# A two-layer attention and state-space decoder: state parameters in ten hooked parts, state data in longer runs, memory values token-major, first channels by contraction tile, norm rows in f32r

## The chip, the cores and the metric

One core of one Trainium2 chip runs the whole program. The metric is the device time of one execution in microseconds (us), as the median of several runs. The engines are TensorE (PE, with its weight loads PEld), VectorE (DVE), ScalarE (ACT), GpSimd (POOL) and SyncE (SP). SP computes nothing here: it issues every transfer of the kernel, in one order fixed at build time.

## The reference

512 tokens of width 1024 pass two layers, and each layer has three residual blocks. Cut to what matters:

```python
for l in range(DEPTH):                                   # 2
    xn = rmsnorm(h, norm_mix_g[l])
    c_q, c_kv, k_r, u = jnp.split(xn @ w_in[l], split_at, axis=-1)
    a_out = mla_group(c_q, c_kv, k_r, ...)               # 8 heads, causal, low-rank q and kv, rotary
    s_out = s5_group(u, lam, log_dt, b, c, d, w_glu, b_glu)
    h = h + concat(rmsnorm(a_out), rmsnorm(s_out)) @ w_out[l]
    h = h + memory_cross_attention(rmsnorm(h), rmsnorm(mem), w_xq, w_xkv, w_xo)   # 256 memory tokens, 4 heads
    h = h + swiglu(rmsnorm(h), w_gate, w_up, w_down)     # inner width 2816
return rmsnorm(h, final_norm_g)

def s5_group(...):                                       # 32 groups of 16 channels, 64 complex states each
    a_bar = jnp.exp(lam * dt); b_bar = ((a_bar - 1) / lam) * b
    states = associative_scan(x[t] = a_bar * x[t-1] + b_bar @ u[t])
    y = Re(c @ states) + d * u; g = gelu(y)
    return y * sigmoid(g @ w_glu + b_glu)
```

## The kernel before

**Layout.** Activations lie channel-major: 128 channels on the partitions, 512 tokens along the free axis, eight such tiles for the width. Every float32 product is three f32r products: each operand is split into a rounded part (`hi`, by ScalarE) and a rest (`lo`, by VectorE, a few by GpSimd), and TensorE adds hi*hi, hi*lo and lo*hi (`mm3`, lines 213 to 218). A weight block is a 128x1024 tile, 512 KB: one transfer into `wraw`, one ScalarE pass (`whi`, L208), one VectorE pass (`wlo`, L209), 24 matmuls, each of them with two buffers.

**Norms.** A norm's row statistics are a column of sums (L289), a scale (L292), a power on GpSimd (L294), and a row that is copied to all partitions (`row`, L276): float32 matmuls of the broadcast column with the identity, two records in the trace for each block of 128 tokens.

**The order of work.** The program is written in source order with priorities, and a planner fixes the order of each engine's queue at build time: an instruction's priority is its place in the source plus an offset (`later`, `OFFS`, `P_OFF`, `PR_UP`, `MS_UP`), and a tile gets a buffer of its tag when one comes free. The state-space work is cut into parts and hung between the 17 attention units `u` by `PLAN` (`x` memory keys and values, `v` state inputs, `m` direct terms, `c` scan, `y` outputs, `G` gelu, `g` gated unit, `s` norm). A part with a negative `u` comes ahead of the units.

**State parameters.** `s5_params` makes, from 1072 columns of parameters per partition, the powers of `a_bar`, the input matrices `BT` (four blocks q, L499, L510), the output matrices `dCA` (four blocks q, L499, L526, with the direct terms by L535), the direct table `dQ` (L541, L542) and the turning table `tab` (L555 to L559). Most of it is VectorE work: products of 128x512 (the helper `bmul`, L562, and the sum, L499). It is called once ahead of layer 0's attention, and once from layer 0's feed-forward block, after the first chunk, for layer 1. While it runs it holds the buffers of tag `s5b`, of which there are six, for parameters and three work tiles; in layer 0 also two for `BT`, which stays on the chip there (in layer 1 it goes through DRAM).

**State data.** The state channels `u` go to DRAM as `du` (L603) and come back as `U2` (L610, eight transfers of 128 KB) with a part of the time steps on the partitions; `U2` has tag `s5b`. The scan's result goes to `W` (L830), the outputs go through `dy` (L868) to `yS` (L872).

**Memory keys and values.** `xkv` makes 16 channel-major blocks of 128x256; VectorE scales them by the memory's norm row (L928). In the cross attention `v_tile` turns the values to token-major by four transposes for each of four tiles (L1036) and splits the result.

**The start.** `load_h` issues eight 256 KB tiles of x with the first weight block of `w_u` behind the first of them; `in_proj` then makes the four blocks of `u` one after the other, each over all eight contraction tiles.

## Time and profile before

| | us |
|---|---|
| median of 3 runs (1619.24 to 1625.9) | 1624.83 |
| the profiled execution | 1616.62 |
| its span, first to last instruction | 1614.8 |
| TensorE busy | 1516.8 (94%) |
| VectorE busy | 914.7 (57%) |
| ScalarE busy | 617.0 (38%) |
| GpSimd busy | 155.0 (10%) |

TensorE's busy time counts pipelined matmuls whose ends are modelled, so 94% doesn't mean that 94% of its best rate is reached: the granted clock of a stretch (1.00 is 2.4 GHz, 0.50 is 1.2 GHz) has to be read beside it. The span falls into these stretches: up to 66 us the first norm and the input projection; 66 to 275 us layer 0's attention with the state-space work; to 380 us its output projection, and the cross attention's start; to about 480 us the rest of the cross attention; to 840 us the feed-forward block; then the same for layer 1, whose attention runs from about 905 to 1070 us.

### The profile page before, as it was taken

To read this page: it belongs to the slowest core of one execution; us is meant where nothing else is said; L and a number is where in the kernel's file an instruction comes from. 1 tells how busy PE (TensorE), PEld (TensorE's weight loads), DVE (VectorE), ACT (ScalarE), POOL (GpSimd) and SP (SyncE) were. 2 spreads that over 40 slices of the span, in tenths; PEclk is the share of its full clock that TensorE was granted. 3 is DMA by queue.
4 is the path that set the end of the run, shared out by engine and by line. 5 is a ranking of instruction groups with operands and counts; after the bars stand their busy time and mean duration, and the time that the engine had idled before them with its cause. 6 is when DMAs were issued, how large, how long until landed. Compare 5 with 4: busy or idle time off the path is not lost.

```text
span 1614.8 us, 20187 instructions
## 1 busy us (share of the span) xinstructions
PE 1516.8 (94%) x8070; PEld 1259.5 (78%) x8070; DVE 914.7 (57%) x1278; ACT 617.0 (38%) x987; POOL 155.0 (10%) x110
## 2 busy tenths in 40 slices
PE   8868898998999999999998889989999999999997
PEld 6647777787878888888886778768888888888886
DVE  6996445757795534445454864555555553443554
ACT  5444365444333223223332455733444322222233
POOL 4310001101001100101100100110000110010111
PEclk9979999999999999999999799989999999999998
DMA  6266634221353222232349363322212223233222
GB/s 219 83 100 128 125 100 156 93 78 53 118 153 107 92 97 99 85 111 92 102 139 169 94 135 110 128 90 92 66 52 88 95 92 104 92 98 98 92 90 75
DMA packets 97630, 169.08 MB, mean 105 GB/s; under 512 B 32640, under 2 KB 55680, under 8 KB 97536
## 3 DMA queue, kind: packets, MB, share of 16 engines
q1 hardware_dynamic: 97536, 167.79, 35.6%
q8 instruction: 63, 1.03, 0.3%
q14 instruction: 31, 0.25, 0.1%
HBM read 150.00 MB, written 15.66 MB: 103 GB/s over the span
## 4 chain that ended last, share of the span: by engine, by line
PE 77%; DVE 7%; DMA 5%; ACT 2%; issue 2%; SPq 2%; POOL 1%; POOLq 0%; ACTq 0%; DVEq 0%
PE mm L215 13%; PE mm L217 13%; PE mm L216 13%; PE f L215 7%; PE f L217 7%; PE f L216 7%; PE mm L744 2%; ACT whi L208 1%; PE f L846 1%; DMA s5b<-dQ 1%; PE t L736 1%; DVE lo L238 1%; DVE wlo L209 1%; DMA wraw<-w_xkv 1%; POOL stat L294 1%
## 5 line engine op out<-in xcount | busy, mean ns | idle before, releaser
L208 ACT ACTIVATE whi<-wraw 128x1024 fp32r<-128x1024 f32 (+1 forms) x234 | 243.3, 1042 | 645.9 <-PE mm L216 299.3
L209 DVE TENSOR_TENSOR wlo<-wraw,whi 128x1024 fp32r<-128x1024 f32 (+2 forms) x228 | 316.5, 1388 | 96.2 <-ACT whi L208 93.9
L215 PE MATMUL mm<-hi,whi 128*128 128x512 f32 x589 | 230.6, 391 | 0.3 <-ACT whi L208 0.3
L217 PE MATMUL mm<-hi,wlo 128*128 128x512 f32 x589 | 229.4, 391 | 0.4 <-DVE wlo L209 0.4
L216 PE MATMUL mm<-lo,whi 128*128 128x512 f32 x589 | 229.3, 390 | 0.0
L215 PE MATMUL mm<-ghi,whi 128*128 128x512 f32 (+1 forms) x368 | 145.7, 396 | 9.2 <-ACT whi L208 7.8
L215 PE MATMUL f<-ghi,whi 128*128 128x256 f32 (+2 forms) x432 | 143.8, 333 | 6.3 <-DVE s5b L928 2.6
L217 PE MATMUL mm<-ghi,wlo 128*128 128x512 f32 (+1 forms) x368 | 145.6, 396 | 2.0 <-DVE wlo L209 1.9
L216 PE MATMUL mm<-glo,whi 128*128 128x512 f32 (+1 forms) x368 | 144.7, 394 | 0.2 <-DVE glo L238 0.2
L217 PE MATMUL f<-ghi,wlo 128*128 128x256 f32 (+2 forms) x432 | 142.5, 330 | 0.8 <-DVE wlo L209 0.8
L216 PE MATMUL f<-glo,whi 128*128 128x256 f32 (+2 forms) x432 | 142.4, 330 | 0.0
L215 PEld LDWEIGHTS mm<-hi,whi 128*128 128x128 f32 x589 | 110.5, 188 | 24.9 <-ACT whi L208 2.2
L217 PEld LDWEIGHTS mm<-hi,wlo 128*128 128x128 f32 x589 | 110.5, 188 | 24.0 <-DVE wlo L209 0.8
L216 PEld LDWEIGHTS mm<-lo,whi 128*128 128x128 f32 x589 | 110.5, 188 | 23.4 <-DVE lo L241 0.5
L1082 POOL TENSOR_TENSOR tmp<-tmp,tmp 128x512 f32<-128x512 f32 x44 | 60.4, 1373 | 573.7 <-DVE tmp L1081 517.4
L215 PE MATMUL f<-hi,whi 128*128 128x512 f32 (+1 forms) x293 | 114.9, 392 | 0.3 <-ACT whi L208 0.3
L217 PE MATMUL f<-hi,wlo 128*128 128x512 f32 (+1 forms) x293 | 114.5, 391 | 0.1
L216 PE MATMUL f<-lo,whi 128*128 128x512 f32 (+1 forms) x293 | 114.4, 390 | 0.0
L933 DVE TENSOR_TENSOR s5b<-mm,s5b 128x512 f32<-128x512 f32 x52 | 35.8, 690 | 114.7 <-PE mm L217 95.2
L237 ACT ACTIVATE hi<-tmp 128x512 fp32r<-128x512 f32 (+1 forms) x100 | 62.8, 630 | 96.4 <-POOL tmp L1082 59.7
L215 PEld LDWEIGHTS f<-ghi,whi 128*128 128x128 f32 (+1 forms) x432 | 82.0, 190 | 16.1 <-DVE tmp L1076 2.8
L215 PEld LDWEIGHTS mm<-ghi,whi 128*128 128x128 f32 (+1 forms) x368 | 69.9, 190 | 25.4 <-ACT whi L208 8.3
(278 smaller groups left out, 2623.6 us busy)
## 6 DMA issues: line engine op xcount, KB each, us to landing
wraw<-w_gate SPq DMA_DIRECT2D x44, 512.0 KB, 3.2
wraw<-w_up SPq DMA_DIRECT2D x44, 512.0 KB, 3.2
wraw<-w_xkv SPq DMA_DIRECT2D x32, 512.0 KB, 3.3
wraw<-w_down SPq DMA_DIRECT2D x30, 448.0 KB, 3.3
wraw<-w_out SPq DMA_DIRECT2D x16, 512.0 KB, 3.3
wraw<-w_xq SPq DMA_DIRECT2D x16, 512.0 KB, 3.2
wraw<-w_xo SPq DMA_DIRECT2D x16, 512.0 KB, 3.2
wraw<-w_down SPq DMA_DIRECT2D x16, 512.0 KB, 3.2
```

What stands on the lines that cost most here:

```text
L208: nc.scalar.activation(hi, raw, AF.Copy)
L209: (eng or nc.vector).tensor_tensor(lo, raw, hi.bitcast(F32), ALU.subtract)
L215: self.nc.tensor.matmul(ps, wh, xh, start=i == 0, stop=False)
L216: self.nc.tensor.matmul(ps, wh, xl, start=False, stop=False)
L217: last = self.nc.tensor.matmul(ps, wl, xh, start=False, stop=i == n - 1)
L237: a = nc.scalar.activation(hi, src, AF.Copy)
L238: b = eng.tensor_tensor(lo, src, hi.bitcast(F32), ALU.subtract)
L294: nc.gpsimd.tensor_tensor(col, ms, self.mhalf[:, :nb], ALU.pow)
L736: nc.tensor.transpose(pt[:, x * 128:(x + 1) * 128], p[ii][:, kb * 128:(kb + 1) * 128], self.ident)
L744: nc.tensor.matmul(po[64 * x:64 * x + 64, cs], vs[kb][:, (2 * pair + x) * 64:(2 * pair + x + 1) * 64], PT[x][:, kk * 256:min(n, kk * 256 + ...
L933: self.nc.vector.tensor_tensor(self.hs[m], ps, self.hs[m], ALU.add)
L1082: nc.gpsimd.tensor_tensor(uf, uf, gf, ALU.mult)
```

## The change

- `s5_params` becomes a generator of ten parts (`s5_gen`): part 0 the powers, parts 1 to 4 the blocks of `BT`, parts 5 to 8 those of `dCA` with their direct terms, part 9 `dQ` and `tab`. In layer 0 parts 0 to 4 stand where all stood, part 5 goes to `u` = -1 and parts 6 to 9 to `u` = 1. For layer 1 the parts hang behind the first gate and up blocks of the feed-forward (`FPLAN`), not behind the first chunk. `BT` goes through DRAM in both layers. Each block q of the direct terms has its own PSUM bank and copy. In layer 1 half of the second-half products of blocks 1 and 3 go to GpSimd (`POOLQ`). The rotary table's four work tiles move from `s5b` to tag `P`.
- `du`, `U2`, `W`, `dy` and `yS` get new layouts: the contiguous runs of `U2`'s load grow from 256 B to 1 KB, those of `W` from 256 B to 2 KB, those of `yS` from 256 B to 512 B; those written to `dy` shrink from 4 KB to 512 B. The number of transfers stays.
- The values of the memory are made token-major: the memory tile is the stationary operand, 256 value columns move. ScalarE scales the result by column, and `v_tile` splits it as it lies, without transposes.
- In layer 0, `w_u0` holds the `u` weights by contraction tile; `in_proj` runs over the contraction tiles with four PSUM banks open, and the four weight transfers stand between the x tiles.
- `row` splits the column into f32r parts (one ScalarE and one VectorE instruction of 128x4) and does two f32r matmuls for each block.
- `PLAN`, `OFFS`, `P_OFF`, `MS_UP` and `IN_POOL` get other values.

```diff
+    out["w_u0"] = wi[0][:, u0:].reshape(4, 2, 128, 512).transpose(0, 2, 1, 3).reshape(4, 128, 1024)
-    POOLQ = ((), ())
-    P_OFF = (150, 2900)
+    POOLQ = ((), (1, 3))
+    P_OFF = (500, 3000)
-    IN_POOL = ((0, 2, 6), ())
+    IN_POOL = ((2, 5), (3, 6))
     PLAN = ((
-        (-1, "x", 0), (-1, "x", 1), (1, "v", 0), (2, "m", 0), (2, "x", 2), (2, "m", 1), (2, "x", 3), (3, "m", 2),
+        (-4, "p", 0), (-4, "p", 1), (-4, "p", 2), (-4, "p", 3), (-4, "p", 4), (-1, "x", 0), (-1, "p", 5),
+        (-1, "x", 1), (-1, "x", 2), (1, "p", 6), (1, "p", 7), (1, "p", 8), (1, "p", 9), (1, "v", 0), (2, "m", 0),
 ...
-        (-2, "v", 0), (-2, "m", 0), (-1, "c", 0), (-1, "c", 1), (0, "m", 1), (0, "x", 0), (0, "x", 1), (0, "y", 0),
+        (-2, "v", 0), (-2, "m", 0), (-1, "m", 1), (-1, "x", 0), (-1, "x", 1), (0, "c", 0), (0, "c", 1), (0, "x", 2),
 ...
+    FPLAN = (0, 0, 1, 1, 1, 1, 1, 1, 2, 5)
-    PR_UP, MS_UP = 1500, 3000
+    PR_UP, MS_UP = 1500, 2300
     def row(self, col):
+        hi, lo = (self.t([128, 4], "cs", F32R)[:, :nb] for _ in range(2))
+        nc.scalar.activation(hi, col, AF.Copy)
+        nc.vector.tensor_tensor(lo, col, hi.bitcast(F32), ALU.subtract)
         for b in range(nb):
-            self.nc.tensor.matmul(ps[:, b * 128:(b + 1) * 128], col[:, b:b + 1].to_broadcast([128, 128]), self.ident,
-                                  start=True, stop=True)
+            for x in (hi, lo):
+                nc.tensor.matmul(ps[:, b * 128:(b + 1) * 128], x[:, b:b + 1].to_broadcast([128, 128]), self.identr,
+                                 start=x is hi, stop=x is lo)
     def rope_tables(self):
-        w = self.t([128, 4, 512], "s5b")
-        posf, ang, k, r = (w[:, i] for i in range(4))
+        posf, ang, k, r = (self.t([128, 512], "P") for _ in range(4))
     def s5_gen(self, l):
-        if l == 0:
-            BT = [x[:, q] for x in [self.t([128, 2, 2, 512], "s5b") for _ in range(2)] for q in range(2)]
-        else:
-            BT = self.dram([4, 128, 2, 512], f"dBT{l}")
+        BT = self.dram([4, 128, 2, 512], f"dBT{l}")
 ...
+            yield
     def in_proj(self, l):
+            for k in range(KT):
+                if k % 2 == 0:
+                    wh, wl = self.pre.pop(0)
+                for m in range(4):
+                    ms = slice((k % 2 * 4 + m) * 128, (k % 2 * 4 + m + 1) * 128)
+                    for w, x in ((wh, 0), (wh, 1), (wl, 0)):
+                        nc.tensor.matmul(pss[m], w[:, ms], X[k][x], start=k == x == 0 and w is wh,
+                                         stop=k == KT - 1 and w is wl)
     def load_u(self, du):
-            nc.sync.dma_start(U2[b * 16:(b + 1) * 16],
-                              du[:, :, 7 - b, :].rearrange("(g c) t j -> c t g j", c=16))
+            nc.sync.dma_start(U2[b * 16:(b + 1) * 16], du[:, 7 - b, :].rearrange("(g c) w -> c g w", c=16))
     def xkv(self, l, X, i):
+                    nc.tensor.matmul(o, xh[:, ts], wh[:, ks], start=hf == tb == k == 0, stop=False)
 ...
+            nc.scalar.activation(self.xv[:, tb, (i - 4) * 256:(i - 3) * 256], ps[:, tb * 256:(tb + 1) * 256], AF.Copy,
+                                 scale=self.mcol[:, tb:tb + 1])
         def v_tile(half, tb):
-            pt = self.p("t")
-            for i in range(4):
-                nc.tensor.transpose(pt[:, i * 128:(i + 1) * 128],
-                                    self.xv[:, half * 4 + i, tb * 128:(tb + 1) * 128], self.ident)
-            return self.split(pt)
+            return self.split(self.xv[:, tb, half * 512:(half + 1) * 512])
```

## Rows read from the trace of the kernel before

**Rows 1.** Windows: stretch and length; busy PE, PEld, DVE, ACT, POOL; clock; DMA share; GB/s.

```profile
0.00:66.00 66.00, 55.50 (x238) 43.32 (x239) 53.00 (x103) 28.93 (x46) 30.64 (x25) 0.95 0.49 168
66.00:132.00 66.00, 42.39 (x363) 32.41 (x362) 56.49 (x91) 29.71 (x57) 6.40 (x5) 0.77 0.59 108
132.00:275.00 143.00, 132.92 (x960) 113.88 (x959) 81.30 (x122) 73.04 (x141) 5.08 (x4) 0.98 0.49 121
380.00:500.00 120.00, 111.73 (x660) 92.34 (x659) 96.86 (x157) 46.66 (x78) 7.78 (x7) 0.97 0.37 114
500.00:850.00 350.00, 349.38 (x1545) 288.12 (x1544) 163.87 (x167) 100.65 (x122) 28.73 (x22) 1.00 0.31 102
850.00:905.00 55.00, 45.93 (x301) 36.96 (x300) 26.61 (x39) 17.28 (x30) 2.38 (x2) 0.84 0.81 157
905.00:1080.00 175.00, 157.81 (x1052) 134.66 (x1052) 103.44 (x156) 93.67 (x177) 16.45 (x6) 0.93 0.41 112
```

**Rows 2.** The chain that ended last, 104 to 132 us: start, length, what.

```profile
107.16 3.17 DMA dCA<-s5b
110.46 0.64 SPq L610
...
115.19 10.10 DMA s5b<-du
...
125.48 1.83 PE s L799 x29
```

**Rows 3.** VectorE's groups by form, 60 to 132 us: busy, mean ns, idle before.

```profile
L499 DVE TENSOR_TENSOR s5b<-s5b,tmps 128x512 f32<-128x512 f32 x16 | 10.7, 680 | 0.0
L562 DVE TENSOR_TENSOR s5b<-s5b,s5b 128x512 f32<-128x512 f32 x8 | 6.5, 816 | 0.0
L562 DVE TENSOR_TENSOR tmps<-s5b,s5b 128x512 f32<-128x512 f32 x8 | 5.9, 741 | 0.0
L558 DVE TENSOR_TENSOR tmps<-s5b 128x512 f32<-128x512 f32 x4 | 4.2, 1041 | 0.0
L555 DVE TENSOR_TENSOR s5b<-s5b 128x1024 f32<-128x1024 f32 x2 | 3.7, 1900 | 0.0
...
L292 DVE TENSOR_SCALAR stat<-t 128x4 f32<-128x4 f32 x2 | 0.3, 148 | 0.0
```

**Rows 4.** The chain that ended last, 856 to 908 us.

```profile
878.07 10.09 DMA tmps<-memT
...
889.59 0.69 DVE tmp L637
```

**Rows 5.** DMA issues of the whole span: count, KB each, median us to landing.

```profile
s5b<-xT SPq DMA_DIRECT2D x2, 1024.0 KB, 7.0
```

**Rows 6.** Windows of the start, columns as in the first group.

```profile
19.10:25.90 6.80, 6.80 (x19) 5.54 (x20) 4.27 (x9) 1.04 (x1) 6.12 (x4) 0.50 0.43 134
```

**Rows 7.** TensorE in order of time, 343 to 347 us: start, length, what.

```profile
343.00 1.05 PE L276 MATMUL t<-const,stat 128*128 128x128 f32 x8
343.88 0.60 PE L1036 MATMUL t<-const,s5b 128*128 128x128 f32 x4
344.24 0.47 PE L217 MATMUL mm<-hi,wlo 128*128 128x512 f32 x1
```

**Rows 8.** TensorE in order of time, 104 to 107.5 us.

```profile
105.09 0.22 PE L716 MATMUL s<-maskr,identr 128*128 128x128 f32 x1
105.15 0.44 PE L217 MATMUL mm<-hi,lo 128*128 128x512 f32 x1
```

**Rows 9.** ScalarE's groups by form, whole span: the smallest copy.

```profile
L325 ACT ACTIVATE identr<-const 128x128 fp32r<-128x128 f32 x1 | 0.3, 298 | 0.0
```

**Rows 10.** SP's waits, 380 to 480 us: total us, times, longest.

```profile
SPq L517 <- ACT tmps L516: 27.5, 7, 11.3
```

**Rows 11.** VectorE in order of time, 84 to 92 us.

```profile
88.53 1.77 DVE L562 TENSOR_TENSOR s5b<-s5b,s5b 128x512 f32<-128x512 f32 x1
```

**Rows 12.** Line 238 on GpSimd: duration ns min/median/max, first and last start us.

```profile
L238 POOL TENSOR_TENSOR lo<-tmp,hi x4: 1311/1576/4692, 85.5 to 916.9; 64x512 fp32r<-64x512 f32 x4
```

More of the change, by code (lines that the diff above doesn't have):

```diff
@@ L126, in lay_out @@
     out["w_xq"] = np.stack([blocks(v["w_xq"][l]) for l in range(L)])
-    out["w_xkv"] = np.stack([blocks(v["w_xkv"][l]) for l in range(L)])
+    out["w_xkv"] = np.stack([blocks(v["w_xkv"][l][:, :DM]) for l in range(L)])
+    xv = v["w_xkv"][:, :, DM:].reshape(L, 2, 4, 128, 4, 256)
+    out["w_xv"] = xv.transpose(0, 4, 1, 3, 2, 5).reshape(L, 8, 128, 1024)
     out["w_xo"] = np.stack([blocks(v["w_xo"][l]) for l in range(L)])
@@ L404, in s5_params, with s5_gen @@
     def s5_params(self, l):
+        gen = self.s5_gen(l)
+        return lambda i: next(gen)
+    def s5_gen(self, l):
         nc, V, P = self.nc, self.nc.vector, self.nc.gpsimd
@@ L607, in load_u @@
         nc = self.nc
-        U2 = self.t([128, 4, 8, 64], "s5b")
+        U2 = self.t([128, 8, 256], "s5b")
         for b in range(8):
-            nc.sync.dma_start(U2[b * 16:(b + 1) * 16],
-                              du[:, :, 7 - b, :].rearrange("(g c) t j -> c t g j", c=16))
-        self.U2 = U2.rearrange("p t g j -> p (t g) j")
+            nc.sync.dma_start(U2[b * 16:(b + 1) * 16], du[:, 7 - b, :].rearrange("(g c) w -> c g w", c=16))
+        self.U2 = [U2[:, q % 8, q // 8 * 64:q // 8 * 64 + 64] for q in range(G)]
     def in_proj2(self, l, X, R):
@@ L809, in s5_scan @@
         if hf == 0:
-            self.W = self.t([128, 32, 64], "s5b")
+            self.W = self.t([128, 2, 1024], "s5b")
         hs = slice(hf * 8, hf * 8 + 8)
@@ L836, in s5_y0 @@
         if q == 0:
-            self.y = self.t([128, 32, 64], "s5b")
+            self.y = self.t([128, 8, 4, 64], "s5b")
         if q % 2 == 0:
@@ L853, in s5_y @@
         if q == 0:
-            self.dy = [self.dram([128, 16, 64], f"dy{l}_{i}") for i in range(2)]
+            self.dy = [self.dram([128, 8, 128], f"dy{l}_{i}") for i in range(2)]
         y, half = self.y, q // 2
@@ L867, in s5_y @@
         dy = self.dy[half]
[L868 removed]
+        hs = slice(half * 128, half * 128 + 128)
+        nc.sync.dma_start(dy, y.rearrange("p g t j -> p g (t j)")[:, :, hs])
         if half == 0:
[L870 removed]
+            self.yS = self.t([128, 8, 256], "s5b")
         for g8 in range(8):
[L872 to L873 removed]
+            nc.sync.dma_start(self.yS[g8 * 16:(g8 + 1) * 16, :, hs],
+                              dy.rearrange("(s c) g w -> g c s w", c=16)[g8])
     def s5_gelu(self, l):
@@ L1136, in run @@
                 self.rope_tables()
-                self.s5_params(0)
+                params = self.s5_params(0)
+                for u, f, i in self.PLAN[0]:
+                    if u == -4:
+                        self.part(params, i, self.OFFS[0].get("p", 0))
             with (self.later(-self.PR_UP) if l == 0 else nullcontext()):
                 self.load_u(du)
+                if l == 0:
+                    for u, f, i in self.PLAN[0]:
+                        if u == -3:
+                            self.part(params, i, self.OFFS[0].get("p", 0))
                 self.in_proj2(l, X, R)
@@ L1154, in run, with hook @@
             self.cross(l)
-            self.ffn(l, lambda: self.s5_params(l + 1) if l + 1 < self.depth else None)
+            params = self.s5_params(l + 1) if l + 1 < self.depth else None
+            def hook(u):
+                for i, x in enumerate(self.FPLAN if params else ()):
+                    if x == u:
+                        self.part(params, i, 0)
+            self.ffn(l, hook)
         self.final()
```

126 lines of the change are left out of this document (69 added, 57 removed), and 10 rows, old and new, of the table PLAN.

## The prediction, made before the changed kernel ran

> **What bounds the kernel now.** I read the page's shares first: TensorE is busy for 94% of the span, so the end is set by its work and by what it loses. The windows [rows 1] say where it loses: busy time times granted clock is work at 2.4 GHz, and the rest of the stretch is lost. In the feed-forward, 500 to 850 us, 349.38 of 350 us at clock 1.00 are work; nothing is to be had there but by taking matmuls away. From 66 to 132 us it is 42.39 x 0.77 = 32.6 of 66 us, so 33 us are lost, the densest loss of the kernel; VectorE is busy for 56.49 of the same 66. From 132 to 275 us 132.92 x 0.98 = 130 of 143 are work, 13 lost. Layer 1's start loses 55 - 45.93 x 0.84 = 16 and its attention 175 - 157.81 x 0.93 = 28. The kernel's start, 0 to 66 us, loses 66 - 55.50 x 0.95 = 13. All other stretches together are small. The chain of waits, read next, names the causes. At layer 0 it runs over VectorE to the last `dCA` transfer (107.16 + 3.17 = 110.33), and only then over eight loads of `U2` (from 110.46 to 115.19 + 10.10 = 125.29) to the state matmuls at 125.48 [rows 2]. `U2` needs nothing of `dCA`; it needs a buffer of the six `s5b` ones, all of which the parameters hold, and SP stands with it. At layer 1 the chain goes over transfers that queue one behind another: a memory tile takes 10.09 us to land, and a VectorE evacuation at 889.59 stands behind its split [rows 4].
>
> **Layer 0's attention, 66 to 275 us.** Three edits meet here. `BT` and the rotary table leave `s5b`, so `U2` finds a buffer when `du` is there. The memory tiles and `x` parts come ahead of most of the parameters. And parts 5 to 9 move behind the first attention units. What moves on VectorE: half of the 16 sums (8 x 0.680 = 5.4 us), the second pass's 16 products (6.5 + 5.9), the table (4.2 + 3.7), together 25.7 us [rows 3], plus small ones. It is not removed: in the new place 25.7 us are added to a stretch where VectorE is busy for 81.30 of 143. So I don't add up stalls, I ask how well the joined stretch can be filled. TensorE's work in it is 32.6 + 130 = 163 us, in 209 us: 78%. VectorE's is 56.49 + 81.30 = 138 us. Two rows show what TensorE reaches beside a busy VectorE: 91% from 132 to 275 us, with VectorE at 57%, and 90% from 380 to 500 us (111.73 x 0.97 of 120) with VectorE at 96.86 of 120, or 81%, under the same parameter work [rows 1]. At 87% the stretch takes 163/0.87 = 187 us and VectorE stands at 74%. That is 22 us less. I take a little under the two rows because the state chain (`v`, `m`, `c`, `y`) now starts behind later parameters. Bounds: 163/0.91 = 179 us, 30 less, and nothing; a loss is the slower rival's, below. What hides the moved work is the 17 us or so of `x` products, three parts of 48 matmuls, and the attention units; if that cover isn't ready, the stall comes back at `u` = 1. The new transfers of `BT`, eight out and eight in, queue on SP ahead of weight loads; I cost them at nothing while two weight tiles lie ready, and price the rest as a rival.
>
> **Longer runs, layer 1's start.** `U2` takes 125.29 - 110.46 = 14.8 us for 1 MB in 256 B runs [rows 2]; 1 MB of x in 2 KB runs lands 7.0 us after its issue [rows 5]. With 1 KB runs I take 6 us less, between 0 and 7.8. In layer 0 that is inside the sum above. In layer 1, 850 to 905 us, the DMA engines are busy for 0.81 of the time [rows 1] and the memory tile waits behind `U2` [rows 4], so I carry 5 us to the end. The loads of `W` and `yS` gain too, the write to `dy` loses its 4 KB runs; SP's issues stay in number. From 905 to 1080 us I take 3 us for these and for `x` parts at -1. Together -8, bounds -17 (both stretches filled to 87%: 185/0.87 = 213 of 230 us) and +4 (the shorter runs of `dy`, and `c` behind -1, delaying `y`).
>
> The Trainium skill, page "DMA: Bandwidth & Descriptors", Specifications, says that transfers under 512 B fall short of line rate and gives some 358 GB/s for a core's HBM side. By that, as an estimate, 1 MB in 1 KB runs would take 3 us instead of 14.8 and layer 1 would gain some 6 us more than I take: 1582 instead of 1588. The trace doesn't agree with that rate here: 1 MB took 7.0 us even in 2 KB runs [rows 5].
>
> **The start.** `u` by contraction tile lets TensorE take 12 matmuls per x tile instead of 3. But it already starts on the first tile, so only the stretch at 1.2 GHz from 19.1 to 25.9 us [rows 6] can go: 6.8 x 0.5 = 3.4 us, and some waits. Against it stand 512 KB weights between the x tiles and one `lo` pass more on VectorE. I take -3, bounds -6 and +2.
>
> **Values token-major.** The products stay the same in number and width. 32 transposes go: eight groups of four, each from 343.88 to 344.24, 0.36 us of TensorE's stream [rows 7]: 8 x 0.36 = -2.8 us, at full clock and in the path. The scale moves from VectorE to two ScalarE copies, hidden while ScalarE is busy for under half. Bounds -2.8 and -1.
>
> **Norm rows.** Now eight records take 343.88 - 343.00 = 0.88 us [rows 7]. An f32r product of 128 columns takes 105.15 - 105.09 = 0.06 us at best [rows 8], so eight take 0.48, at worst the same 0.88. For 14 rows that is 0 to -5.6; I take -3. The two new instructions (at most 0.298 and about 0.148 us [rows 3, 9]) with two hand-overs add some 0.5 us to the norm's chain, and ScalarE's queue may stand before them. This shows only where TensorE waits for the row, at four places: the attention norm of both layers and the two last norms: 4 x 0.5 = +2. Net -1, bounds -4 and +6.
>
> **Layer 1's parameters.** Their `BT` writes already stand between 380 and 480 us [rows 10], ahead of the feed-forward in whose source they are called: the planner runs them when an engine is free, and an earlier place changes little. GpSimd takes 12 products from VectorE: 12 x 0.68 = 8 us less in a stretch at 81%, beside slower POOL work. I take 0, bounds -6 and +9.
>
> **Sum.** -22 - 8 - 3 - 2.8 - 1 + 0 = -36.8 us. The profiled execution took 1616.62 us (its span 1614.8), so it would take 1579.8. The median of the runs is 8.2 us above it; with the same distance the changed kernel's median is 1588. The terms' bounds, not all at once, make 1568 to 1602.
>
> **Rivals.**
>
> *The stall only moves.* Parts 6 to 9 stand together at `u` = 1, and TensorE's queue holds their matmuls in order, as it did before; if the joined stretch reaches 82% instead of 87%, it takes 199 us and gains 10: 1600. For it: 25.7 us of VectorE work in a row. Against: the row of 90% beside the same work.
>
> *The buffers don't come free.* Parameters with three work tiles, `U2` and the attention's output make six; the first key tile then finds no `s5b` buffer until part 8 is through, and the `x` cover is missing. Then only the wait for `U2` goes, some 12 us: 22 - 12 = 10 us worse, 1598. For it: that is just how `U2` waits now. Against: the attention's output is first written late.
>
> *GpSimd slows VectorE.* Beside GpSimd's work a product took 1.77 us instead of 0.68 [rows 11], and a GpSimd pass took 4.692 us at worst instead of 1.311 [rows 12]. If all 12 products went like that, 12 x 4.692 = 56 us, in which VectorE does 0.68/1.77 of its work, it would lose 35 us, less the 8 that it is spared: +27 if none of its slack in that stretch takes it up, so 1615. The Trainium skill, page "GPSIMD Engine Reference", Key points, has the rule: both engines share SBUF interfaces, and VectorE instructions with two SBUF inputs contend. Against: 1.77 is the worst row; the mean of that group is 816 ns [rows 3].
>
> *SP stands (slower).* In layer 1, SP stood for 27.5 us in front of seven `BT` writes, waiting for their copies [rows 10]. Now the same writes stand in layer 0's queue, ahead of `w_xkv`, `w_uq` and memory loads. Should all of it reach TensorE, the 22 us don't come and 27.5 us are added: 1588 + 22 + 27.5 = 1637. It decides from about 15 us on: then the whole gain of 37 is gone. For it: one queue in fixed order. Against: two weight tiles are always ahead, and TensorE lost little to SP in layer 1.
>
> **How the numbers follow.** Forecast 0.50; the stall moves 0.20; buffers 0.10; GpSimd 0.07; SP stands 0.13, of which 0.08 end slower and 0.05 near no change. A measurement of this kernel can tell 0.5%, 8.1 us, from no change, so faster means below 1616.7. That holds for the forecast and the first two rivals, and for 0.03 of GpSimd's: 0.83. Within: 0.04 + 0.05 = 0.09. Slower: 0.08. The range reaches down to 1562, where the best ends of several terms meet, and up to 1616, the GpSimd rival; outside it I leave SP's 0.13 and a little below.
>
> **What would show it.** Right: the `U2` loads of layer 0 are issued before the last `dCA` write; no TensorE gap of 6 us before the state matmuls; 66 to the end of attention some 20 us shorter at a clock above 0.77; the memory transposes gone; `U2` of layer 1 landed in under 9 us; TensorE's wait before the attention norm's row longer by under 1 us. Wrong: VectorE over 85% busy in layer 0's attention with TensorE waiting on parameter sums; waits of SP for `BT` copies with weights landing late; products on GpSimd beyond 2 us each with long VectorE rows beside them; or a first attention unit that starts no earlier than now.

## The result, and the profile after

The changed kernel takes **1596.12 us** (median of 4 runs, 1595.12 to 1603.26) beside 1622.78 us for the kernel before (4 runs). The ratio is 0.9846, with a 95% interval of 0.9809 to 0.9883: 25 us less, by the ratio. The profiled execution took 1595.71 us, its span 1593.9; before, the span was 1614.8, so the two traces differ by 20.9 us.

Both traces can be cut at the same pieces of work. The cuts are instructions of VectorE: the start of the last query evacuation and of the division of a layer's last pair of heads, and the end of a block's last full-width residual (the last feed-forward has four half-width ones behind it).

| stretch | before, us | after, us | difference | forecast |
|---|---|---|---|---|
| start, to the last query evacuation | 69.7 | 61.3 | -8.4 | -3 |
| layer 0: to the last pair of heads | 198.9 | 200.7 | +1.8 | -22 |
| output projection | 59.6 | 57.6 | -2.0 | 0 |
| cross-attention | 133.0 | 127.6 | -5.4 | -1.4 |
| feed-forward | 370.8 | 373.5 | +2.7 | 0 |
| layer 1: to the first attention score | 88.5 | 86.9 | -1.6 | -8 together with the next |
| to the last pair of heads | 134.2 | 126.5 | -7.7 | |
| output projection | 61.8 | 58.1 | -3.7 | 0 |
| cross-attention | 122.6 | 121.0 | -1.6 | -1.4 |
| feed-forward | 354.5 | 357.3 | +2.8 | 0 |
| after the last full-width residual | 21.2 | 23.4 | +2.2 | about +1 |

The forecast's largest term did not come. The windows of the kernel after show it (stretch and length; busy PE, PEld, DVE, ACT, POOL; clock; DMA share; GB/s), most of them in the edges of [rows 1]:

```profile
0.00:61.30 61.30, 52.85 (x247) 42.21 (x248) 50.46 (x106) 30.98 (x52) 28.36 (x24) 1.00 0.68 198
...
66.00:132.00 66.00, 53.07 (x468) 45.08 (x466) 60.37 (x95) 30.12 (x57) 5.23 (x4) 0.86 0.52 153
132.00:275.00 143.00, 129.80 (x871) 108.61 (x868) 80.77 (x127) 77.22 (x156) 6.93 (x5) 0.89 0.50 123
61.30:262.00 200.70, 174.97 (x1316) 147.59 (x1315) 137.27 (x212) 105.32 (x208) 10.15 (x7) 0.91 0.54 141
...
262.00:319.60 57.60, 54.12 (x223) 43.92 (x224) 40.54 (x79) 26.24 (x39) 8.82 (x5) 0.88 0.24 81
...
850.00:905.00 55.00, 48.10 (x322) 37.92 (x321) 37.81 (x58) 25.42 (x44) 7.76 (x5) 0.84 0.63 134
905.00:1080.00 175.00, 167.41 (x1088) 140.96 (x1088) 99.69 (x150) 99.01 (x188) 6.72 (x4) 0.98 0.43 122
```

and the windows of the kernel before that answer to 0 to 61.3, 61.3 to 262 and 262 to 319.6 us:

```profile
0.00:69.70 69.70, 57.60 (x249) 44.77 (x250) 56.67 (x109) 30.25 (x48) 32.82 (x25) 0.95 0.49 167
...
69.70:268.60 198.90, 167.03 (x1258) 138.63 (x1256) 128.44 (x201) 97.88 (x191) 9.10 (x7) 0.91 0.51 111
...
268.60:328.20 59.60, 55.76 (x276) 45.97 (x277) 46.09 (x85) 30.18 (x43) 10.26 (x5) 1.00 0.37 124
```

From 66 to 132 us TensorE now does 53.07 x 0.86 = 45.6 us of work instead of 32.6: 13 us gained, as meant, though a part of it only because the work stands 8 us earlier. From 132 to 275 us it does 129.80 x 0.89 = 115.5 instead of 130: 14.5 us given back. Cut at the pieces of work, the attention stretch holds 174.97 x 0.91 = 159 us of work in 200.7 us, or 79%, after 167.03 x 0.91 = 152 in 198.9, or 76%. It is a little fuller and not shorter, since a part more of the memory projection fell into it. The output projection behind it has as much less, 54.12 x 0.88 = 47.6 us after 55.8, but it too runs at a lower clock and gets only 2 us shorter. VectorE is no busier than before from 132 to 275 us (80.77 against 81.30 us), and none of TensorE's longest waits there is for it.

The two stretches have to be read together, since work moved from one to the other. They take 258.3 us after 258.5. TensorE stands idle in them for 258.3 - 174.97 - 54.12 = 29.2 us instead of 258.5 - 167.03 - 55.76 = 35.7: 6.5 us of waits did go. But the clock columns say that it loses 174.97 x 0.09 + 54.12 x 0.12 = 22 us to stretches at 1.2 GHz instead of 167.03 x 0.09 = 15. What the waits gave, the clock took.

Which waits went and which came shows in TensorE's waits of the attention stretch (total us, times, longest), in the kernel before from 69 to 269 us and then in the changed one from 61 to 262 us, and in the record at 149.98 us (start, length):

```profile
PE s L799 <- DMA s5b<-du: 6.7, 1, 6.7
PE s L535 <- DVE s5b L499: 5.7, 3, 2.3
...
PE f L846 <- DMA s5b<-dQ: 2.4, 1, 2.4
```

```profile
PE f L867 <- issue: 5.3, 1, 5.3
PE mm L220 <- DVE tmp L720: 5.1, 1, 5.1
PE s L820 <- DMA raw<-dBT: 3.6, 2, 2.3
```

```profile
149.98 2.37 PE L867 MATMUL f<-s5b,s5b 128*128 128x64 f32 x10 [5.32 <-issue]
```

The old wait for `U2` (L799) is gone: its eight loads are issued from 52.6 to 56.0 us and landed by 63.2, where they were issued at 110.46 and later [rows 2]. The waits for the parameter sums (L535) are gone too. The wait for `dBT` (L820) is new, and the one for `dQ`, which went through DRAM in the kernel before as well, grew from 2.4 us (L846) to 5.3 (L867). Waits for state data and parameters from DRAM were 6.7 + 2.4 = 9.1 us and are 5.3 + 3.6 = 8.9: one kind took the place of the other. The chain of waits from 95 to 160 us goes over them:

```profile
126.27 4.58 DMA raw<-dBT
...
141.81 7.06 DMA s5b<-dQ
...
149.98 3.65 PE f L867 x16
```

and the DMA queues of 125 to 152 us (the queue's packets, MB and share of the 16 engines; then issues, count, KB each, median us to landing) say why they take long:

```profile
q1 hardware_dynamic: 4477, 5.04, 89.8%
...
raw<-dBT SPq DMA_DIRECT2D x4, 256.0 KB, 4.7
s5b<-dQ SPq DMA_DIRECT2D x8, 128.0 KB, 5.6
...
dQ<-s5b SPq DMA_DIRECT2D x1, 480.0 KB, 6.5
```

The DMA engines are busy for 89.8% of these 27 us: the `dQ` write (6.5 us), its eight loads, the `dBT` reads and weights share them.

The wait of 5.1 us for VectorE (L720) ends at 84.27 us, ahead of the first attention unit; from 62 to 90 us VectorE is busy for 26.01 of 28 us. The chain of waits goes there over a write of `dBT`, behind which a parameter product (L573) stands on VectorE:

```profile
79.44 2.00 DMA dBT<-tmps
81.50 0.10 DVE tmps L573
...
83.52 0.70 DVE tmp L720
```

TensorE's longer stretches at half clock begin in or right behind its gaps (columns as in the windows above):

```profile
130.50:140.70 10.20, 9.04 (x78) 7.91 (x79) 8.44 (x15) 3.16 (x7) 0.00 (x0) 0.50 0.92 245
147.60:157.80 10.20, 7.82 (x32) 6.87 (x33) 3.38 (x9) 2.69 (x6) 0.00 (x0) 0.50 0.19 29
82.70:89.50 6.80, 5.23 (x19) 4.01 (x20) 6.74 (x12) 3.26 (x6) 0.00 (x0) 0.50 0.08 17
263.60:277.30 13.70, 11.96 (x37) 9.40 (x38) 9.79 (x18) 6.22 (x12) 1.25 (x2) 0.50 0.01 3
```

The first of these follows the waits for `dBT` (126 to 131 us), the second begins in the gap before L867, the third in the gap that ends at 84.27 us. The last lies in the output projection, which had the full clock before. At half clock the 9.04 + 7.82 us of busy time are worth 8.4: as much again is lost as in the gaps.

At layer 1, 850 to 905 us gives 48.10 x 0.84 = 40.4 us of work against 38.6, and 905 to 1080 us 167.41 x 0.98 = 164 against 147: here the forecast's sign and place hold. These windows begin some 11 us later in the work than those of the kernel before, so the table is the better measure: -1.6 and -7.7 us, where -8 was forecast for both.

### The profile page after: what moved, and what is told of

Read it like the earlier page. It is cut to its first block, busy times and chain, and to the rows that moved or that the text cites. A ratio compares the mean times of both kernels' runs of the same rounds, so it can differ in the third digit from the quotient of the medians.

```text
span 1593.9 us, 20203 instructions
## 1 busy us (share of the span) xinstructions
PE 1519.3 (95%) x8038; PEld 1258.6 (79%) x8038; DVE 908.6 (57%) x1274; ACT 627.0 (39%) x1027; POOL 169.7 (11%) x123
## 4 chain that ended last, share of the span: by engine, by line
PE 83%; DVE 6%; DMA 4%; ACT 4%; issue 1%; SPq 1%; POOL 0%; DVEq 0%; ACTq 0%; POOLq 0%
PE mm L220 14%; PE mm L222 13%; PE mm L221 13%; PE f L220 7%; PE f L222 7%; PE f L221 7%; PE mm L768 2%; DVE lo L243 1%; PE t L760 1%; DVE wlo L214 1%; DMA s5b<-dQ 1%; ACT whi L213 1%; PE f L961 1%; PE f L962 1%; PE f L963 1%
## 5 line engine op out<-in xcount | busy, mean ns | idle before, releaser
L214 DVE TENSOR_TENSOR wlo<-wraw,whi 128x1024 fp32r<-128x1024 f32 (+1 forms) x227 | 312.6, 1378 | 99.0 <-ACT whi L213 96.5
L220 PE MATMUL mm<-ghi,whi 128*128 128x512 f32 (+1 forms) x352 | 138.3, 393 | 1.6 <-DVE tmp L1108 0.8
L222 PE MATMUL mm<-ghi,wlo 128*128 128x512 f32 (+1 forms) x352 | 138.7, 394 | 0.0
L221 PEld LDWEIGHTS mm<-lo,whi 128*128 128x128 f32 x580 | 108.9, 188 | 22.4
L220 PE MATMUL f<-ghi,whi 128*128 128x512 f32 (+1 forms) x304 | 107.0, 352 | 8.1 <-DVE s5b L950 2.4
L220 PE MATMUL f<-hi,whi 128*128 128x512 f32 x286 | 112.7, 394 | 1.6 <-DVE glo L243 1.4
L222 PE MATMUL f<-hi,wlo 128*128 128x512 f32 x286 | 111.9, 391 | 0.4 <-DVE wlo L214 0.4
L221 PE MATMUL f<-lo,whi 128*128 128x512 f32 x286 | 111.8, 391 | 0.0
L221 PE MATMUL f<-glo,whi 128*128 128x512 f32 (+1 forms) x304 | 106.6, 351 | 0.2 <-DVE glo L243 0.2
L222 PE MATMUL f<-ghi,wlo 128*128 128x512 f32 (+1 forms) x304 | 106.5, 350 | 0.3 <-DVE wlo L214 0.3
L222 PEld LDWEIGHTS mm<-ghi,wlo 128*128 128x128 f32 (+1 forms) x352 | 66.1, 188 | 14.8 <-DVE tmp L1108 0.3
```

The costliest lines, as they stand in the source:

```text
L214: (eng or nc.vector).tensor_tensor(lo, raw, hi.bitcast(F32), ALU.subtract)
L220: self.nc.tensor.matmul(ps, wh, xh, start=i == 0, stop=False)
L221: self.nc.tensor.matmul(ps, wh, xl, start=False, stop=False)
L222: last = self.nc.tensor.matmul(ps, wl, xh, start=False, stop=i == n - 1)
```

## The experiments

Each kernel's time is compared by its ratio to the kernel before, run on the same chip beside it (medians of 1620.92 to 1623.57 us).

### Undoing one part: the rows

`row` as before (float32 matmuls of the column with `ident`), all else as changed:

```diff
-        nc.scalar.activation(hi, col, AF.Copy)
-        nc.vector.tensor_tensor(lo, col, hi.bitcast(F32), ALU.subtract)
...
+            self.nc.tensor.matmul(ps[:, b * 128:(b + 1) * 128], col[:, b:b + 1].to_broadcast([128, 128]), self.ident,
+                                  start=True, stop=True)
```

> The changed kernel with the norm rows back in float32 and nothing else undone. Theory A (the prediction's term): the f32r rows give 1 us in all (3 us less TensorE work, 2 us for the longer chain), so this takes 1597 where the changed one took 1596, and the stages keep their lengths within 1 us each. Rival B: the longer chain costs more than the products save, since the changed trace shows TensorE waiting for the two new instructions before ten rows and the two last norms end 2.2 us later after the last residual than before; then this is 2 to 5 us faster, 1591 to 1594, and the stretch from the last residual to the end is 2 us shorter (21.2 instead of 23.4 us).

Measured: **1608.38 us**, 0.992 [0.9886, 0.9954], 12 us more than the changed kernel. Both theories missed. But the matmuls didn't get cheaper in f32r. The groups of the row's matmuls (busy, mean ns, idle before), after and then with the rows undone (where the memory's column, four records of 0.6 us in all, is a group of its own):

```profile
L285 PE MATMUL t<-identr,cs 128*128 128x128 f32 x124 | 22.4, 318 | 7.9 <-ACT cs L280 5.4 <-DVE cs L281 2.5
```

```profile
L281 PE MATMUL t<-const,stat 128*128 128x128 f32 x120 | 20.1, 318 | 9.0 <-POOL stat L299 9.0
```

So the 12 us had to come from somewhere else, and three more kernels went after them.

### The rows alone, in the kernel before

The same edit the other way round: `row` of the changed kernel in the kernel before, nothing else.

```diff
+        hi, lo = (self.t([128, 4], "cs", F32R)[:, :nb] for _ in range(2))
+        nc.scalar.activation(hi, col, AF.Copy)
+        nc.vector.tensor_tensor(lo, col, hi.bitcast(F32), ALU.subtract)
```

> The kernel before with one edit: the norm rows go through TensorE in f32r as in the changed kernel, all else as it was. Theory A (the rows themselves are cheaper, so that the 12 us that the changed kernel lost when its rows were put back are the rows' own): 1622 - 12 = 1610 us. Theory B (the rows' matmuls are not cheaper: in the profiles 124 records take 22.4 us in f32r against 20.1 us in f32; what was lost was the planner's order, which any edit of a duration shuffles): within 8 us of before, 1614 to 1630, with another order of the work and 2 us more at the end of the kernel, where nothing covers the two added instructions.

Measured: **1627.56 us**, 1.0028 [1.0006, 1.005]: the rows alone cost 4 us. The rows' own work is the same as in the changed kernel:

```profile
L280 PE MATMUL t<-identr,cs 128*128 128x128 f32 x124 | 22.2, 314 | 11.5 <-ACT cs L275 6.3 <-DVE cs L276 5.2
```

What follows the last full-width residual grew from 21.2 to 23.4 us here too. Theory B holds: the rows are no gain of their own.

### The f32 rows again, with one order changed

With the rows undone, GpSimd's queue had its two copies of `bd` ahead of the power that the kv norm waits for. GpSimd in order of time, 50 to 63 us, with the rows undone, and then in the changed kernel:

```profile
52.05 8.76 POOL L494 COPY s5b<-s5b 64x512 f32<-64x512 f32 x2 [9.48 <-DVE s5b L485]
60.89 1.01 POOL L299 TENSOR_TENSOR stat<-stat,mhalf 128x4 f32<-128x4 f32 x1
```

```profile
52.25 1.13 POOL L303 TENSOR_TENSOR stat<-stat,mhalf 128x4 f32<-128x4 f32 x1 [10.75 <-DVE stat L301]
53.33 7.01 POOL L498 COPY s5b<-s5b 64x512 f32<-64x512 f32 x2
```

The edit to the kernel with f32 rows moves these copies to ScalarE:

```diff
-            P.tensor_copy(bd[rr, :, :, g2, :], bb[rr])
+            if l == 0:
+                nc.scalar.activation(bd[rr, :, :, g2, :], bb[rr], AF.Copy)
+            else:
+                P.tensor_copy(bd[rr, :, :, g2, :], bb[rr])
```

> The kernel of u_rows (the changed kernel with f32 rows, 1608.4 us) with layer 0's two copies into the block-diagonal buffer on ScalarE instead of GpSimd. In u_rows the copies were ordered ahead of the kv norm's power on GpSimd (8.76 us, power at 60.89 us) and in the changed kernel behind it (power at 52.25 us). Theory A (what the f32 rows lost is the order of the work, and half of it this one place): the last query evacuation comes back from 67.9 to about 62 us and the end by some 6 us, to 1600 to 1603 us. Theory B (the f32 rows themselves cost the 12 us, place by place): 1606 to 1610 us.

Measured: **1599.2 us**, 0.9856 [0.9837, 0.9876]. With f32 rows still in place 9 of the 12 us are back, so most of the loss hangs on the order of the work and not on the rows themselves. The place was guessed wrong, though: the last query evacuation came only from 67.9 to 66.3 us, since the power, now alone on GpSimd, took 5.54 us:

```profile
54.84 5.54 POOL L299 TENSOR_TENSOR stat<-stat,mhalf 128x4 f32<-128x4 f32 x1 [12.43 <-DVE stat L297]
```

The rest came in layer 0's attention, 208.4 to 202.5 us for the same work: with the rows undone its window has 180.35 us busy at clock 0.87, with the copies moved 174.94 at 0.91, both 157 to 159 us of work. Why the other order keeps the clock up I did not settle.

### Undoing one part: the first channels

```diff
-                    if k % 2 == 0:
-                        self.pre.append(self.load_w(self.A["w_u0"][2 * b + k // 2]))
+                    if b == k == 0:
+                        self.pre.append(self.load_w(self.A["w_u"][0, 0]))
...
-        if l == 0:
-            pss = [self.p(t) for t in ("mm", "mm", "f", "s")]
-            for k in range(KT):
...
```

With this loop out, layer 0 takes the branch of layer 1, one output block after the other.

> The changed kernel with the first channels of layer 0 by output block again, as before the change. Theory A (the prediction's term): the contraction tiles gave 3 us, so 1599. Rival B: they gave more; in the changed trace the last block of the input projection is evacuated at 61.3 us instead of 69.7, and the slow clock at 19 to 26 us is gone, so this evacuation comes back to 68 to 70 us and the time is 1602 to 1605. Rival C: the 8 us are there but attention gives them back, because VectorE and not TensorE sets its pace there: the evacuation at 68 to 70 us and the time within 3 us of 1596.

Measured: **1605.61 us**, 0.9895 [0.9871, 0.9919]: 8 us or so more than with the change. The last query evacuation is back at its old 69.7 us, and the first attention score comes at 97.0 instead of 90.1.

### Undoing one part: the values

Memory values channel-major again, with 16 transposes for each layer in the cross-attention and the scale by the memory's norm row back on VectorE. Cut to the transposes:

```diff
-            return self.split(self.xv[:, tb, half * 512:(half + 1) * 512])
+            pt = self.p("t")
+            for i in range(4):
+                nc.tensor.transpose(pt[:, i * 128:(i + 1) * 128],
+                                    self.xv[:, half * 4 + i, tb * 128:(tb + 1) * 128], self.ident)
+            return self.split(pt)
```

> The changed kernel with the memory values channel-major again: 32 transposes back, the scale on VectorE. Theory A (the prediction's term): 2.8 us slower, 1599, all of it between the end of the output projection and the end of the cross attention of the two layers, 1.4 us each. Rival B: the freed transposes also freed PSUM banks and VectorE, the cross attention of layer 0 got 5.4 us shorter in the changed kernel (133.0 to 127.6 us): then 4 to 6 us slower, 1600 to 1602.

Measured: **1603.2 us**, 0.9877 [0.9855, 0.9899], some 5 us more. The transposes themselves are a part of it (this kernel's group of layer 0: count, busy, mean ns):

```profile
L1057 PE MATMUL t<-const,s5b 128*128 128x128 f32 x16 | 2.3, 274 | 0.0
```

Layer 0's cross-attention goes from 127.6 to 134.9 us, layer 1's only from 121.0 to 121.5, though both have the same transposes. The windows of layer 0's, first with the values undone, then of the changed kernel:

```profile
323.40:458.30 134.90, 126.07 (x674) 106.09 (x672) 86.94 (x145) 55.37 (x105) 18.77 (x15) 0.99 0.24 80
```

```profile
319.60:447.20 127.60, 123.52 (x658) 104.13 (x657) 85.37 (x146) 55.35 (x105) 18.43 (x15) 0.99 0.26 85
```

TensorE's busy time differs by 2.6 us, its idle time by 134.90 - 126.07 - (127.60 - 123.52) = 4.7 us. TensorE's longest wait in the first of these is for VectorE's scaling of the probabilities; the like wait of the changed kernel is 0.2 us:

```profile
PE t L1040 <- DVE P L1033: 2.7, 2, 2.4
```

So it is VectorE that comes late there, and the next layer's parameters lie on it beside this stretch. That the transposes and the split behind them push its queue back is likely, not shown.

### Undoing one part: the longer runs

```diff
-        du = self.dram([128, 8, 256], f"du{l}")
+        du = self.dram([128, 4, 8, 64], f"du{l}")
...
-            nc.sync.dma_start(U2[b * 16:(b + 1) * 16], du[:, 7 - b, :].rearrange("(g c) w -> c g w", c=16))
+            nc.sync.dma_start(U2[b * 16:(b + 1) * 16],
+                              du[:, :, 7 - b, :].rearrange("(g c) t j -> c t g j", c=16))
```

and `W`, `y`, `dy` and `yS` likewise in their old layouts.

> The changed kernel with the old layouts of the state data (256 B runs for the reloads). Theory A (the prediction's terms): 8 us in layer 1's start and attention and some in layer 0's, so 1604 to 1608, with layer 1's reload of the state channels taking 13 us from first issue to last landing instead of 10. Rival B: layer 1's 13 us came from the order of its parts and not from the runs: then 1596 to 1600, with layer 1's attention as short as in the changed kernel.

Measured: **1595.95 us**, 0.9835 [0.9811, 0.9858]: no difference. The transfers did get shorter. The loads of `U2` in layer 1 (SP's issue ns min/median/max; then us to landing min/median/max), after and then with the old runs:

```profile
L635 SPq DMA_DIRECT2D s5b<-du x8: 332/430/431, 848.9 to 852.1; - x8
...
DMA to landing us min/median/max: 3.5/5.4/7.3
```

```profile
L635 SPq DMA_DIRECT2D s5b<-du x8: 605/632/1002, 851.6 to 856.3; - x8
...
DMA to landing us min/median/max: 4.0/6.5/8.8
```

From the first issue to the last landing that is 852.1 + 7.3 - 848.9 = 10.5 us against 856.3 + 8.8 - 851.6 = 13.5, and the page's count of packets under 512 B falls from 32896 to 16512. Half of these 3 us is SP's issuing: 852.1 - 848.9 = 3.2 us from the first issue to the last, against 856.3 - 851.6 = 4.7. None of it reaches the end.

The Trainium skill, "DMA: Bandwidth & Descriptors", Specifications, has transfers under 512 B short of line rate; the direction agrees with what is left of the 3 us here, the estimate of 3 us for the whole 1 MB, worked out from the rate of that page, doesn't, with 10.5 us measured.

### Moving the hooked parts: all ahead

All ten parts of layer 0 stand ahead of the attention. The entries of `PLAN` that move:

```diff
-        (-1, "p", 5),
+        (-4, "p", 5), (-4, "p", 6), (-4, "p", 7), (-4, "p", 8), (-4, "p", 9),
...
-        (1, "p", 6), (1, "p", 7), (1, "p", 8), (1, "p", 9),
```

> The changed kernel with all ten parameter parts of layer 0 ahead of the attention: parts 5 to 9 go from behind the first units to the place of parts 0 to 4. Theory A (the prediction's: spreading the parts fills layer 0's attention): the stall before the state matmuls comes back, 16 us or more are lost, 1612 us or above, first score later by 10 us or more. Theory B (the attention stretch gained nothing from the parts' new place, since what U2 gained was lost again at the round trips through dBT and dQ): 1590 to 1602 us.

Measured: **1597.16 us**, 0.9849 [0.9819, 0.988]: the same as with the parts spread. The first attention score comes at 104.9 instead of 90.1 us, as theory A had it, and yet nothing is lost at the end, as theory B had it. TensorE's waits from 64 to 200 us and the window of its attention stretch:

```profile
PE s L544 <- DVE s5b L509: 6.0, 2, 5.4
...
PE s L820 <- DMA raw<-dBT: 5.0, 1, 5.0
```

```profile
64.80:269.60 204.80, 174.97 (x1305) 146.18 (x1303) 133.94 (x211) 104.48 (x207) 10.81 (x8) 0.92 0.52 137
```

The stretch is 4 us longer than with the spread parts, and the parameter sums (L509) stand in the waits again; the wait for `dQ` (L867) is gone, since `dQ` is written earlier. One wait is traded for the other. The 4 us and those of a later start (64.8 against 61.3 us) come back behind it, in pieces of 0.5 to 3 us.

### Moving the direct terms behind a memory part

The entries of `PLAN` that move:

```diff
-        (2, "m", 0), (2, "m", 1), (2, "x", 3), (3, "m", 2),
+        (2, "x", 3), (3, "m", 0), (3, "m", 1), (3, "m", 2),
```

> The changed kernel with the first two tiles of layer 0's direct terms (m) moved one attention unit later, behind a part of the memory projection, so that the loads of dQ have time to land. Theory A (the TensorE gap of 5.3 us at 144 to 150 us, behind the dQ round trip, and the half-clock stretch after it of 10.2 us, are on the path): 5 to 9 us less, 1587 to 1591 us. Theory B (the stretch is short of ready work and another wait takes its place): 1594 to 1600 us, with a gap of like size elsewhere between 130 and 190 us.

Measured: **1597.26 us**, 0.9849 [0.9823, 0.9875]. Theory A is out: the wait before L867 doesn't go, it grows. The time is theory B's, but the gap is at the same place, where B had it elsewhere. TensorE's waits from 120 to 190 us:

```profile
PE f L867 <- DMA raw<-dBT: 9.6, 1, 9.6
PE f L867 <- DMA s5b<-dQ: 2.8, 1, 2.8
```

A later place in the plan gives TensorE nothing to do meanwhile. There was too little ready work around 140 us in either of the two orders.

### Giving layer 1's parameter products back to VectorE

```diff
-    POOLQ = ((), (1, 3))
+    POOLQ = ((), ())
```

> The changed kernel with the parameter products of layer 1's two sub-parts given back from GpSimd to VectorE. Theory A (GpSimd spares VectorE 12 x 0.68 us in a stretch where VectorE is the busiest): 1604 us, feed-forward of layer 0 longer by some 8 us. Theory B (the feed-forward of layer 0 is bound by TensorE and hides VectorE's work): 1592 to 1600 us.

Measured: **1589.66 us**, 0.98 [0.9774, 0.9826], better than both theories. GpSimd's products in the changed kernel took (ns min/median/max, first and last start us):

```profile
L573 POOL TENSOR_TENSOR s5b<-s5b x2: 1804/2008/2211, 393.7 to 412.2; 128x512 f32<-128x512 f32 x2
...
L573 POOL TENSOR_TENSOR tmps<-s5b,s5b x2: 1420/2694/3967, 452.4 to 465.5; 128x512 f32<-128x512 f32 x2
```

That is 2.0 and 2.7 us in the mean, where VectorE's products of this size took 0.82 and 0.74 us [rows 3]. But layer 0's cross-attention and feed-forward, where they ran, stay as they were without them (127.8 and 373.6 us against 127.6 and 373.5). The difference lies later, 126.5 to 123.4 us in layer 1's attention and 357.3 to 355.7 in its feed-forward, where the edit changes only the order of the work. And layer 1's attention takes 123.6 to 124.3 us in four kernels that keep the products on GpSimd (values and runs undone, all parts ahead, direct terms later), so those 3 us aren't owed to this edit. The edit is a gain; that GpSimd's slowness is its cause is not shown.

### The last norm's rows in f32, on top of it

```diff
+        self.f32row = True      # in final: row takes the f32 form
```

> The changed kernel with layer 1's parameter products back on VectorE, and with the norm rows of the last norm alone in f32 as before (nothing else lies beside them). Theory A (the two added instructions are on the path where nothing covers them: the tail went from 21.2 to 23.4 us): 2 us less than the 1589.7 us with the products on VectorE, 1587.5 us, the tail back at 21 us. Theory B (the tail is bound by the output's way out, not by the rows): 1589.7 us.

Measured: **1588.46 us**, 0.9785 [0.9767, 0.9803], the best of all. The median alone can't tell it from the kernel without this edit, but the tail can: 21.1 us after the last full-width residual instead of 22.9. Its waits for the row, in the changed kernel and then here:

```profile
PE t L285 <- DVE cs L281: 2.3, 1, 2.3
PE t L285 <- ACT cs L280: 1.8, 2, 1.3
```

```profile
PE t L281 <- POOL stat L310: 2.2, 2, 1.1
```

4.1 us against 2.2: theory A.

### The copies on ScalarE, on top of that

The edit of the copies above, in the best kernel.

> The kernel of u_last32 with layer 0's two copies into the block-diagonal buffer on ScalarE instead of GpSimd, where they take 7 us at 53 us, beside a busy VectorE. Theory A (GpSimd's queue in front of the norms' powers costs the start nothing as long as the power stands ahead of the copies, as it does here): within 2 us of u_last32, 1586 to 1590 us. Theory B (the copies slow VectorE, which is busy for 9.8 of 10 us there, by the access that both share): 3 to 6 us less, 1582 to 1585 us.

Measured: **1591.35 us**, 0.9805 [0.9788, 0.9822], 3 us more than without and a little beyond theory A's range; theory B is out. From 50 to 62 us TensorE is busy for all 12 us with either. The same edit that gave 9 us back with f32 rows costs 3 here, where the power already stands ahead of the copies.

### First channels and values alone, in the kernel before

The two edits whose undoing cost 8 and 5 us, put into the kernel before; plan, parameters, runs and rows as before.

```diff
+    out["w_u0"] = wi[0][:, u0:].reshape(4, 2, 128, 512).transpose(0, 2, 1, 3).reshape(4, 128, 1024)
...
-            self.mm_block(self.A["w_xkv"][l, m], X, ps[:, m % 2 * MEM:m % 2 * MEM + MEM],
+                    nc.tensor.matmul(o, xh[:, ts], wh[:, ks], start=hf == tb == k == 0, stop=False)
```

> The kernel before with two edits alone: first channels by contraction tile, memory values token-major; plan, parameters, runs and rows as before. Theory A (these two are the gain, each worth in the old plan what its undoing cost in the new one, 8 and 5 us): 1622.8 - 13 = 1610 us. Theory B (they pay only together with the new plan of the parts): 1615 to 1625 us.

Measured: **1609.36 us**, 0.9912 [0.989, 0.9934], 14 us less than before: the total is theory A's. Place by place it is so for the values, with the cross-attention at 127.7 us in layer 0 and 120.9 in layer 1 after 133.0 and 122.6. The first channels bring the last query evacuation only from 69.7 to 66.3 us, not to 61.3, and the rest lies in stretches that neither edit touches: layer 0's feed-forward 7.5 us longer, layer 1's output projection 4.7 shorter. So the total doesn't show that each edit is worth in the old plan what its undoing cost in the new one.

## Why the prediction was right or wrong

The time was forecast as 1588 us, within 1562 to 1616, faster by over 0.5%; it is 1596. Range and sign held. The sum didn't come about in the way that its terms said, and the largest failed. By the traces the change is worth 20.9 us, where the sum had 36.8. That the median is only 8 us off is in part luck: the sum was carried to a median 8.2 us above the profiled execution, and the changed kernel's median lies 0.4 us above its own. Two of the signs named failed as well: `U2` of layer 1 took 10.5 us to land, not under 9, and layer 0's attention ended 268.6 - 262 = 6.6 us earlier, not some 20.

**Layer 0's attention, -22, measured +1.8.** The step that failed is the fill of 87%, taken "a little under the two rows" of 91% and 90%. Measured were 79% and 200.7 us, 42 of them lost. The fill of two windows was carried over to a joined stretch whose first part is short of ready work: from 62 to 90 us VectorE is busy for 26.01 of 28 us and TensorE for 20.13, at clock 0.76. And its state chain had been given a round trip through DRAM for `BT`, with that of `dQ` now right ahead of its use. The text costed the 16 transfers of `BT` "at nothing while two weight tiles lie ready", which looks at weights alone. Weights were in time: TensorE's longest wait for one in the stretch is 1.1 us. The `dBT` and `dQ` data were not: 8.9 us of waits, and 8.4 us for the two half-clock stretches that begin there, 17 of the 42. The clock stands in the term only inside the fill of the two rows (0.98 and 0.97 there); here it was 0.91, and 0.88 in the output projection, and that took back the 6.5 us of waits that went. That the round trips alone keep the stretch from 87% isn't shown: no kernel left `BT` on the chip, and the later place for `dQ`'s readers won nothing.

The rival "the stall only moves" gave 199 us for this stretch and 1600 in all. Its effect is what happened, for the most part by another mechanism: not VectorE's sums at `u` = 1 but a VectorE that is late ahead of the first unit, DMA round trips under engines that are 89.8% busy, and half-clock stretches after both. That spreading the parts as such brings nothing at the end is shown by the kernel with all ten ahead.

**The start, -3, measured -8.4.** The term counted the stretch at 1.2 GHz, 3.4 us at most, "and some waits", and those were the larger share. The stretch lost 69.7 - 57.60 x 0.95 = 15 us before and 61.3 - 52.85 = 8.5 after, and the last query evacuation has 2 us less of other work ahead of it. Undoing it cost 8 us at the end, and the bound of -6 was too narrow. But beside the old plan and rows the same edit moves this evacuation by 3.4 us only, which is the term; the rest needs what else was changed ahead of it, and which part of that it needs isn't shown.

**The values, -2.8, measured 5 by the undoing.** The transposes show 2.3 us busy in layer 0, where the sum had 1.4 for a layer; missing was what stands behind them in layer 0's cross-attention, 4.7 us of idle time.

**Longer runs and layer 1, -8, measured -9.3 up to the last pair.** The number fits, its reason doesn't. With the old runs the kernel is as fast, and its layer 1 goes as well (87.6 and 124.3 us in place of 86.9 and 126.5). `U2` gained 3 us where 6 were taken, and none of it was on the path. As undoing the values or the rows leaves layer 1's start and attention as short too (83.6 and 123.7 us, 86.7 and 126.7), the gain there is left to the new plan with its offsets and to the new place of the layer's parameters; no kernel undid those by themselves.

**The rows, -1, measured: none of their own.** Work was forecast at -3 and is +2 to +3 of busy time (22.4 us, against 19.5 before and 20.7 with the rows undone, for 124 records each). The step that failed is reading a pitch of 0.06 us from a stream of other products: the row's own records follow each other by some 0.11 us in either form, as the last section shows. The chain's cost was right in size and not in place: forecast were +2 at four places, and +2.2 us came in the tail alone, while TensorE's idle time before all rows is 7.9 us, after 11.5 in the kernel before. Alone the rows cost 4 us.

**Layer 1's parameters, 0, measured +6.5** by the undoing, within the bounds of -6 and +9, with the cause open.

**The other rivals.** The buffers came free: `U2` was loaded at 52.6 us. SP stood for `BT` copies, 11.7 us in 5 waits from 60 to 160 us, without weights coming late. GpSimd's products were slow without VectorE's stretch getting longer.

**The sum.** The first channels and the values, put alone into the kernel before, give 14 of the 25 us. Of the other 11 the runs and the spreading give none, and the kernels without GpSimd's products and without the tail's f32r rows are 6.5 and some 2 us faster. If the parts added up, some 19 us would be left for the rest: state buffers freed, `BT` through DRAM, the new plan and its offsets. It was not divided further, and the parts need not add up. How much order alone can do is seen in the f32 rows: 12 us lost, 9 of them back by two copies on another engine.

## What to carry to other kernels

A fill that one stretch reaches is no estimate for another: ask first what its products wait for, and when a change sends data through DRAM that was held on the chip, count the write, the read and the load on the DMA engines at that moment, for the one who reads it, not only for the weights behind it. Count the clock along with the waits: a stretch can lose fewer microseconds to waiting and as many more to 1.2 GHz. A part of a large change is worth what its undoing shows only if the order of the rest stays: put it alone into the old kernel too, and where the two disagree, as the rows' -12 and +4 us did, the order was measured along with the edit. A shorter transfer, or an earlier one, is a gain only where the next wait isn't already standing behind it.

## What the hardware showed that was not expected

A power of 128x4 elements on GpSimd took 1.01 us, 1.13 us and 5.54 us in three kernels at 52 to 61 us. VectorE did nothing beside the first, was busy throughout beside the second, and for 5.30 of 5.60 us beside the third. The two copies of 64x512 took 7.01 to 8.76 us there beside a busy VectorE, nearly all of it in the first of the two, and 1.3 us together on ScalarE. In the kernel before the same two took 1.00 and 0.97 us at 54.6 us, with VectorE busy throughout, and the mean of its four was 886 ns:

```profile
L485 POOL COPY s5b<-s5b 64x512 f32<-64x512 f32 x4 | 3.5, 886 | 14.4 <-DVE s5b L476 14.3
```

The prediction had 4.692 us as GpSimd's worst row, for 512 elements a partition [rows 12]. What makes the same small instruction five times as long isn't settled; that VectorE is busy beside it isn't enough.

An f32r row, two products for each block of 128 tokens, was hardly cheaper for TensorE than the float32 one, which leaves two records for each block. Eight records where nothing is waited for, in the changed kernel and then with the rows undone:

```profile
334.65 1.00 PE L285 MATMUL t<-identr,cs 128*128 128x128 f32 x8
350.56 1.05 PE L281 MATMUL t<-const,stat 128*128 128x128 f32 x8
```

The last of the eight starts 0.73 us after the first in f32r and 0.78 us after it in float32.
